# Feed-forwards that begin with half the tokens, memory keys beside the products, mixing norms two steps forward

## The chip, the cores and the metric

The kernel runs on one core of one Trainium2 chip. The metric is device time in microseconds (us), from launch to end, as the median of several executions; lower is better. Five engines work side by side and wait for each other through semaphores: PE (TensorE, matrix products and transposes), DVE (VectorE) and ACT (ScalarE) for elementwise work, POOL (almost idle here) and SP, which only issues transfers (DMA) here.

## The reference

One layer of a decoder over 1024 tokens of width 1024, all in f32, with pre-normalisation everywhere (`rmsnorm(x, g) = x * rsqrt(mean(x*x) + eps) * g`):

```python
h = x + 0.5 * swiglu(rmsnorm(h, ffn1_norm), w_gate, w_up, w_down)      # feed-forward 1, width 2816
u = rmsnorm(h, mix_norm)
(fq, fk, fv, ff, dq, dk, dv, iq, ik, iw, mq, g) = split(u @ w_in)
o_a = fox_attention(fq, fk, fv, logf)                                  # causal, with forget bias
o_b = dsa_attention(dq, dk, dv, iq, ik, iw, k_sel)                     # top-k keys by an indexer
km, vm = split(rmsnorm(mem, mem_norm) @ w_mem_kv)                      # 256 memory tokens
o_c = memory_attention(mq, rmsnorm(km, mem_k_norm), vm)
h = h + (sum_i sigmoid(g_i) * (o_i @ w_branch_i)) @ w_out
h = h + 0.5 * swiglu(rmsnorm(h, ffn2_norm), ...)                       # feed-forward 2
# swiglu(x, wg, wu, wd) = (silu(x @ wg) * (x @ wu)) @ wd
```

## The kernel before

Every f32 factor of a product is split into a high part (a rounded copy that PE takes at full rate, made by an ACT cast) and a low part (the rest, made by a DVE subtraction), and a product is three matmuls: high by high, high by low, low by high. In the rows `wH`, `wL` are the parts of weights (rings of four buffers, fed by staging tiles `wS`), `th`, `tl` those of activations, `nT` the PSUM tile that a transpose fills, and a 128x512 matmul is the unit of nearly all work.

**Feed-forward.** `FeedForward.first_half` computes gate and up, `second_half` the down product. Both use a fast scheme with seven half-size products in place of eight. For gate and up the token-side factors are seven tiles of 128 x (4 x 512), made once per feed-forward by `Combos`: B11 and B21 are the first 512 tokens (rows 0 to 3 of eight rows of 128 tokens), lower and upper half of the width; B12 and B22 are the last 512 tokens (rows 4 to 7); T3 = B22 - B12, T2 = T3 + B11, T1 = B12 - B11, T4 = B21 - T2. The weight-side sums are the tiles `S`, made by DVE for each job (`prep_sums`, `prep_split`). A job is one 2 x 128-column piece of gate or up; there are 22 jobs, each of seven products (`product`), each product of 12 matmuls. The map from product to token tile is

```python
RIGHT = {1: B11, 2: B21, 3: B22, 4: T4, 5: T1, 6: T2, 7: T3}
```

and a job goes 1, 2, 6, 5, 7, 3, 4. The results of a job pass through PSUM banks `gx`, `gy` into an SBUF tile `gu` by ACT copies and DVE additions. Jobs 0 and 1 are interleaved product by product, as their token tiles become ready; the others follow each other.

**Before feed-forward 1** the kernel of before normalises and turns (transposes) the memory rows, multiplies them by `w_mem_kv` (96 matmuls, tile `tm`, consumers `mem_keys` and `mem_values`), and between these normalises the rows of x in pairs (t, t+4), `x_pair`, each pair turned by `Combos.sums`, which writes all of the token tiles for those 128 columns. Only when all four pairs are through do `open_high` and `first_half` begin: the first product waits for all eight rows.

**Before feed-forward 2** the product with `w_out` runs over the eight token rows in the order 0, 4, 1, 5, 2, 6, 3, 7 (consumer `residual`), each row is normalised as it ends, and the pairs are turned in the same way.

**Between feed-forward 1 and the mixing**, `second_half` calls `beside(i, y)` at its last steps (42 steps in all; i = 0 at step 30). At i = 8 to 11 it normalises rows 0 to 3 for the mixing (`to_mix`, `norm_rows`: a scale, eight transposes into free PSUM banks, a split); at i = 11 it issues the loads of the narrow projection's weights (`nb.fetch`). After the second half come row 3's rest, the narrow projection (tile `nar`, 192 matmuls of 128x256) and, as filler, gate products.

The order of work is the order of issue in the program, smoothed by a scheduler within each engine; a planner class (`_Flow`) keeps estimated clocks only to choose which of several chains is issued next. Engines run their own lists in order.

Of the kernel before, what the change touches and what calls it, by code (L numbers as in the profile page):

```python
# [19 lines left out]
P = 128  # L20
# [135 lines left out]
def trunk_layer_kernel(  # L156
# [133 lines left out]
    def normalise(tp, out, row, gain):  # L290
        v = tp.tile([P, 1], F32, tag="nv", name="nv", bufs=3)
        junk = out
        if out is row:
            junk = tp.tile([P, D], BF16, tag="njunk", name="njunk", bufs=1)
        A.activation(junk, row, AF.Square, accum_out=v)
        y = rsqrt_mean(tp, v, D)
        V.scalar_tensor_tensor(out, row, y[:, 0:1], gain, op0=OP.mult, op1=OP.mult)


    def norm_rows(tp, row, gain, uh, ul, t, free=None, sq=None):  # L300
        sq = sq() if sq else tp.tile([P, D], F32, tag="nsq", name="nsq", bufs=2)
        normalise(tp, sq, row, gain)
# [18 lines left out]
    class Block:  # L321


        def __init__(self, bp, srcs, ncols, bufs=4, tag="b", out=None):
            self.bp, self.srcs, self.ncols, self.bufs, self.tag, self.out = bp, srcs, ncols, bufs, tag, out
            self.ws, self.ready = [None] * len(srcs), [0.0] * len(srcs)
# [8 lines left out]
        def step(self, uh, ul, t, consume, after=None):  # L335
# [7 lines left out]
            for k in range(NK):  # L343
                wh, wl = self.ws[k // kper]
                wh, wl = wh[:, k % kper], wl[:, k % kper]
                a, b = uh[:, k, t * P:(t + 1) * P], ul[:, k, t * P:(t + 1) * P]
# [34 lines left out]
    class Combos:  # L381


        def __init__(self):
            self.lp = pool("tl", side="right")
            self.low = [self.lp.tile([P, 4, 512], F32, tag=f"t{i}", name="raw", bufs=1) for i in range(7)]

        def open_high(self):
            self.hp = pool("th", side="right")
            high = self.hp.tile([P, 8, 4, 512], F32R, name="th")  # L390
            self.high = [high[:, i] for i in range(7)]
            self.spare = lambda: high[:, 7]


        def sums(self, tp, t, ra, rb):
            sl = slice(t * P, (t + 1) * P)
            bs = []
            for r in (ra, rb):
                for c in range(2):
                    pt = bank("nT")  # L400
                    for k in range(4):
                        T.transpose(pt[:, k * P:(k + 1) * P], r[:, (4 * c + k) * P:(4 * c + k + 1) * P], ident)
                    bs.append(pt.rearrange("p (k t) -> p k t", k=4))
            b11, b21, b12, b22 = bs
            low = [x[:, :, sl] for x in self.low]
            x12 = tp.tile([P, 4, P], F32, tag="x12", name="x12", bufs=1)
            A.copy(x12, b12)
            A.copy(low[B11], b11)
            V.tensor_sub(low[T3], b22, x12)
            A.copy(low[B21], b21)  # L410
            V.tensor_sub(low[T1], x12, b11)
            A.copy(low[B22], b22)
            V.tensor_add(low[T2], low[T3], b11)
            V.tensor_sub(low[T4], b21, low[T2])


        def split(self, i):
            hi, raw, self.low[i] = self.high[i], self.low[i], self.spare()
            A.copy(hi, raw)
            V.tensor_sub(self.low[i], raw, hi.bitcast(F32))  # L420
            self.spare = lambda: self.lp.tile([P, 4, 512], F32R, tag=f"t{i}", name="tl", bufs=1)

        def release(self):
            self.hp.release()
            self.lp.release()

    class FeedForward:
        def __init__(self, combos, w_gate, w_up, w_down, residual):
            self.staged, self.ready = {}, {}
            self.c, self.wgu, self.wd, self.residual = combos, (w_gate[0], w_up[0]), w_down[0], residual  # L430
            self.raw, self.jobs, self.n_jobs = {}, {}, 2 * HF
# [11 lines left out]

        def fetch(self, j):
            if j < self.n_jobs and j not in self.raw:
                p, w = j // 2, self.wgu[j % 2]
                rs = []
                for f in (p, p + HF):
                    r = slot([P, NK, P], F32, "wS")
                    load(r, w[:, f * P:(f + 1) * P].rearrange("(k p) f -> p k f", p=P))  # L450
                    rs.append(r.rearrange("p (a k) f -> p a (k f)", a=2))
                self.raw[j] = rs

        def job_of(self, j):
            if j not in self.jobs:
                self.jobs[j] = self.tp.tile([P, 4, 512], F32, tag="S", name="S", bufs=2), {}
            return self.jobs[j]

        def prep_sums(self, j, part):
            ra, rb = self.raw[j]  # L460
            s = self.job_of(j)[0]
# [7 lines left out]
        def prep_split(self, j, g):  # L469
            ra, rb = self.raw[j]  # L470
            s, d = self.job_of(j)
            v, names = ((ra, (1, 2)), (s[:, 0:2], (6, 5)), (s[:, 2:4], (7, 3)), (rb[:, 1:2], (4,)))[g]
# [4 lines left out]
        def product(self, pt, j, n, start):  # L477
            sh, sl = self.jobs[j][1][n]
# [6 lines left out]
        def job(self, j):  # L485
            gate = j % 2 == 0
            u = self.tp.tile([P, 4, 512], F32, tag="gu", name="gu", bufs=3)
# [12 lines left out]
            x = tagged_bank("x", 2, "gx")  # L500
            self.product(x, j, 1, True)
            yield
            y = tagged_bank("y", 4, "gy")
            self.product(y, j, 2, True)
# [5 lines left out]
            y = tagged_bank("y", 4, "gy")  # L510
# [19 lines left out]
            del self.raw[j], self.jobs[j]  # L530


        def first_half(self):
            fl.sync()
            self.tp = pool("ffa")
            c = self.c
            for j in range(2):
                self.fetch(j)
                self.prep_split(j, 0)
            pair = [self.job(0), self.job(1)]  # L540

            def step(split=(), groups=()):
                for i in split:
                    c.split(i)
                for g in pair:
                    next(g)
                for g in groups:
                    for j in range(2):
                        self.prep_split(j, g)

            c.split(B11)
            step()
            c.split(B21)
            for j in range(2):
                self.prep_sums(j, 0)
                self.prep_split(j, 1)
            step((T2,))
            step((T1,))
            for j in range(2):
                self.prep_sums(j, 1)  # L560
                self.prep_split(j, 2)
            step((T3,))
            step((B22,), (3,))
            self.fetch(2)
            self.fetch(3)
            step((T4,))
            for part in range(2):
                self.prep_sums(2, part)
                self.prep_split(2, part)
            step()  # L570
            self.prep_split(2, 2)
            last = pair
            for j in range(2, self.n_jobs):
                g, n = self.job(j), j + 1
                for st in range(7):
                    next(g)
# [210 lines left out]
    def head_norm(tp, pt, nh, bufs=4):  # L787
        hd = 512 // nh
        sq = tp.tile([P, 512], F32, tag="hx", name="hsq", bufs=bufs)
# [30 lines left out]
    def mem_keys(tp):  # L820
        def consume(t, pt):
            xn = head_norm(tp, pt, 4, 2)
            yield
            for i, v in enumerate(turn(tp, xn)):
                store(km_s[:, :, i].rearrange("h p m -> p h m")[:, :, t * P:(t + 1) * P], v)
        return consume

    def mem_values(tp):
        def consume(t, pt):
# [883 lines left out]
```

## Time and profile before

| | |
|---|---|
| median of 3 runs | 2542.94 us (2538.59 to 2545.95) |
| profiled execution, its own time | 2544.91 us |
| its span, first to last instruction | 2542.9 us |
| PE busy | 2419.0 us, 95% |
| DVE, ACT busy | 64%, 45% |
| instructions | 31538 |

How to read it: the span is the profiled execution's time less 2.0 us that lie outside its instructions. PE is busy nearly all the time, so time can only be won where PE waits or where its clock is low; the waits lie at a few places, and the rows further down show three of them.

### The profile page before, as it was taken

Reading aid. Unit: us, or ns where it says so; the run is one execution under the profiler, and the core shown is the slowest. Engines: PE = TensorE matmul, PEld = TensorE weight load, DVE = VectorE, ACT = ScalarE, POOL = GpSimd, SP = SyncE. Lnnn points to the kernel's source line nnn. Section 1 sums busy time; section 2 is a strip of 40 time slices with the busy share of each in tenths; the row PEclk is TensorE's granted clock in tenths of the full one; section 3 lists DMA queues with packets and bytes.
Section 4 is the critical chain, followed back from the end, with each engine's and each line's share of the span. In section 5 each row is a group of like instructions: output and inputs, shape, how many; then the busy total and the mean of one; then the engine's idle time right before and its main releaser. Section 6 shows DMA issues by size and latency. Waiting matters only on the chain.

```text
span 2542.9 us, 31538 instructions
## 1 busy us (share of the span) xinstructions
PE 2419.0 (95%) x11532; PEld 2001.3 (79%) x11532; DVE 1617.0 (64%) x3201; ACT 1147.4 (45%) x1904; POOL 2.2 (0%) x40
## 2 busy tenths in 40 slices
PE   6999999999999999989899998999979999999998
PEld 4788888888787877778688886877768888888887
DVE  7755555488757588584565556777376555554885
ACT  5533333333433277768865555543144333333332
POOL 0000000000000000000000000000000000000000
PEclk9999999999999999999899999999989999999999
DMA  7222222474334534544455535757422222225743
GB/s 233 75 84 77 88 86 79 157 303 137 128 114 138 156 116 137 151 155 146 132 148 141 149 107 182 233 172 232 175 75 67 91 75 84 91 77 192 269 152 126
DMA packets 297899, 351.63 MB, mean 138 GB/s; under 512 B 18792, under 2 KB 199688, under 8 KB 297744
## 3 DMA queue, kind: packets, MB, share of 16 engines
q1 hardware_dynamic: 297744, 349.62, 42.8%
q8 instruction: 90, 1.47, 0.2%
q14 instruction: 65, 0.53, 0.1%
HBM read 254.98 MB, written 93.54 MB: 137 GB/s over the span
## 4 chain that ended last, share of the span: by engine, by line
PE 79%; DVE 9%; ACT 6%; DMA 3%; issue 3%; SPq 0%; ACTq 0%; DVEq 0%
PE gx L51 19%; PE gy L51 14%; PE tm L51 9%; PE gate L51 8%; PE dx L51 8%; PE dy L51 7%; PE br L51 4%; ACT junk L51 3%; PE po L51 2%; PE pT L51 2%; PE sp L51 2%; DVE wL L51 2%; PE nar L51 1%; PE isc L51 1%; DMA wS<-in_w_in 1%
## 5 line engine op out<-in xcount | busy, mean ns | idle before, releaser
L51 ACT CAST wH<-wS 128x1024 fp32r<-128x1024 f32 x238 | 225.6, 953 | 304.7 <-PE gy L51 103.0
L51 PE MATMUL gx<-th,wH 128*128 128x512 f32 x880 | 317.4, 393 | 7.2 <-ACT th L51 7.2
L51 DVE TENSOR_TENSOR wL<-wS,wH 128x1024 fp32r<-128x1024 f32 x238 | 260.3, 1099 | 98.3 <-ACT wH L51 93.8
L51 PE MATMUL gx<-th,wL 128*128 128x512 f32 x704 | 274.9, 390 | 0.0
L51 PE MATMUL gy<-th,wH 128*128 128x512 f32 x528 | 206.3, 391 | 1.2 <-ACT th L51 1.2
L51 PE MATMUL gy<-tl,wH 128*128 128x512 f32 x528 | 205.4, 389 | 0.0
L51 PE MATMUL gx<-tl,wH 128*128 128x512 f32 x528 | 205.4, 389 | 0.0
L51 PE MATMUL gy<-th,wL 128*128 128x512 f32 x528 | 205.4, 389 | 0.0
L51 PE MATMUL tm<-wH,uh 128*128 128x512 f32 x496 | 199.8, 403 | 3.1 <-ACT wH L51 3.1
L51 PEld LDWEIGHTS gx<-th,wH 128*128 128x128 f32 x880 | 166.9, 190 | 42.8 <-ACT th L51 8.0
L51 PE MATMUL tm<-wL,uh 128*128 128x512 f32 x496 | 196.5, 396 | 2.1 <-DVE wL L51 1.3
L51 PE MATMUL tm<-wH,ul 128*128 128x512 f32 x496 | 196.5, 396 | 0.0
L51 ACT ACTIVATE junk<-wk,sn 128x384 bf16<-128x384 f32 (+5 forms) x186 | 164.2, 883 | 64.6 <-DVE sn L51 55.4
L51 ACT CAST wH<-S 128x1024 fp32r<-128x1024 f32 x88 | 92.4, 1051 | 171.2 <-PE gy L51 167.9
L51 DVE TENSOR_TENSOR wL<-S,wH 128x1024 fp32r<-128x1024 f32 x88 | 107.5, 1223 | 87.3 <-ACT wH L51 87.3
L51 DVE TENSOR_TENSOR gu<-gu,gy 128x512 f32<-128x512 f32 x88 | 60.3, 686 | 157.0 <-PE gy L51 85.3
L51 DVE TENSOR_TENSOR pl<-pT,ph 128x512 fp32r<-128x512 f32 (+1 forms) x176 | 109.5, 637 | 78.9 <-ACT ph L51 77.8
L51 PE MATMUL gate<-uh,wH 128*128 128x512 f32 x384 | 156.0, 406 | 0.0
L51 PEld LDWEIGHTS gx<-th,wL 128*128 128x128 f32 x704 | 133.0, 189 | 27.8
L51 PE MATMUL gate<-uh,wL 128*128 128x512 f32 x384 | 152.5, 397 | 0.0
L51 PE MATMUL gate<-ul,wH 128*128 128x512 f32 x384 | 152.0, 396 | 0.0
L51 PE MATMUL dx<-wH 128*128 128x512 f32 x352 | 137.5, 391 | 3.5 <-DVE rows L51 2.5
(261 smaller groups left out, 5160.9 us busy)
## 6 DMA issues: line engine op xcount, KB each, us to landing
wS<-in_ffn_w_down SPq DMA_DIRECT2D x70, 512.0 KB, 4.7
wS<-in_w_in SPq DMA_DIRECT2D x48, 512.0 KB, 4.0
wS<-in_ffn_w_gate SPq DMA_DIRECT2D x44, 512.0 KB, 3.9
wS<-in_ffn_w_up SPq DMA_DIRECT2D x44, 512.0 KB, 3.7
hid_s<-gu SPq DMA_DIRECT2D x44, 512.0 KB, 3.0
a<-hid_s SPq DMA_DIRECT2D x30, 512.0 KB, 9.5
g_s<-sg SPq DMA_DIRECT2D x48, 256.0 KB, 2.4
bg<-g_s SPq DMA_DIRECT2D x48, 256.0 KB, 3.1
```

The lines of the kernel that those rows point to most:

```text
L51: return fn(*a, **k)
```

## The change

1. `normalise` takes a list of rows with one chain of small rsqrt operations for all of them; rows of x are now normalised in pairs (0,1), (2,3), (4,5), (6,7).
2. Both feed-forwards begin with products 1 and 2 of jobs 0, 1 and 2 (`first_products`, `second_products`, 72 matmuls), which need only rows 0 to 3. Rows 4 to 7 are normalised and turned while these run. `Combos.first(t)` copies a row's two halves into B11 and B21; `Combos.second(t)` makes T3 and T2 per row; T1 and T4 are made later as whole tiles of 128 x 2048 (`rest`). B11 and B21 are split in quarters, T2 in halves (`split(i, parts)`).
3. Memory keys and values are no longer made before feed-forward 1. A generator `mem_kv` is advanced once per product of jobs 4 and up in feed-forward 1's gate and up part; it takes staging tiles from the ring `S`, weight parts from the rings `wH`, `wL`, and two PSUM banks. It issues 12 matmuls at a time between products, at eight places. To make room `gu` has two buffers instead of three in this feed-forward, and `gy` three banks instead of four.
4. `w_out` goes through the rows in order 0 to 7 in feed-forward 2's beginning; row 7's sum and normalisation come after the first products are issued.
5. `beside` starts two steps earlier: norms at i = 6 to 10, narrow weights at i = 9, the first gate weights at i = 10 and 11. Staging tiles for these rows come from the other pool `wx`.

```diff
+    def normalise(tp, outs, rows, gain, tag="njunk", bufs=1):
+        v = tp.tile([P, n], F32, tag="nv", name="nv", bufs=3)
+        for i, (out, row) in enumerate(zip(outs, rows)):
...
+            A.activation(junk, row, AF.Square, accum_out=v[:, i:i + 1])
         y = rsqrt_mean(tp, v, D)
-        V.scalar_tensor_tensor(out, row, y[:, 0:1], gain, op0=OP.mult, op1=OP.mult)
+        for i, (out, row) in enumerate(zip(outs, rows)):
+            V.scalar_tensor_tensor(out, row, y[:, i:i + 1], gain, op0=OP.mult, op1=OP.mult)
...
+        def first(self, t, row):
             sl = slice(t * P, (t + 1) * P)
+            for i, b in zip((B11, B21), self.turned(row)):
+                A.copy(self.raw[i][:, :, sl], b)
+        def second(self, t, row):
+            b12, b22 = self.turned(row)
+            raw = {i: x[:, :, t * P:(t + 1) * P] for i, x in self.raw.items()}
+            A.copy(raw[T1], b12)
+            V.tensor_sub(raw[T3], b22, raw[T1])
+            A.copy(raw[B22], b22)
+            V.tensor_add(raw[T2], raw[T3], raw[B11])
+        def rest(self, i):
+            r = self.raw
+            if i == T1:
+                V.tensor_sub(r[T1], r[T1], r[B11])
+            else:
+                r[T4] = r[T2]
+                V.tensor_sub(r[T4], r[B21], r[T2])
...
+        def first_products(self):
+            self.three = [self.job(j, True) for j in range(3)]
+            for g in self.three:
+                next(g)
+        def second_products(self, beside):
+            for i, g in enumerate(self.three):
+                next(g)
+                beside(i)
...
+                    if beside and j > 3:
+                        self.st = st
+                        next(beside, None)
...
+    def mem_kv(ff):
+        stage = lambda: ff.tp.tile([P, 4, 512], F32, tag="S", name="mS", bufs=2)
...
+                for half in range(2):
+                    yield from until((4, 6)[half])
+                    wh, wl = ff.split2(e[:, 2 * half:2 * half + 2])
+                    yield from until((5, 0)[half])
+                    if acc is None:
+                        acc = [bank("kv") for t in range(2)]
+                    for t in range(2):
+                        for k in range(2):
...
+                            mm3(acc[t], [(a, wh[:, k]), (a, wl[:, k]), (b, wh[:, k])], kt == 0, kt == NK - 1)
...
-    fl.run(order + kv[3:], width=3)
...
+    nm(0, 1)
+    combos.first(0, rows[0])
+    combos.first(1, rows[1])
+    nm(2, 3)
+    ff.begin(1)
+    combos.first(2, rows[2])
+    combos.first(3, rows[3])
+    combos.split(B11, 4)
+    ff.begin(3)
+    ff.first_products()
+    ff.rest()
+    combos.split(B21, 4)
+    nm(4, 5)
+    nm(6, 7)
...
+    ff.second_products(halves)
     nmp.release()
-    ff.first_half()
+    ff.first_half(mem_kv(ff))
...
-        if i == 6:
+        if i == 5:
...
-        if i >= 8:
-            next(m["norms"][i - 8])
-        if i >= 9:
-            next(m["norms"][i - 9], None)
-        if i == 11:
+        if 6 <= i <= 9:
+            next(m["norms"][i - 6])
+        if 7 <= i <= 10:
+            next(m["norms"][i - 7], None)
+        if i == 9:
...
-        consume.order = (0, 4, 1, 5, 2, 6, 3, 7)
...
+    combos.split(B11, 4)
+    combos.split(B21, 4)
+    total(NT - 1, final[0])
...
+    ff.first_products()
+    ff.rest()
+    normalise(tp, [h[NT - 1]], [h[NT - 1]], gain3)
+    ff.second_products(lambda i: combos.second(3, h[NT - 1]) if i == 0 else None)
```

How the engines' lists move, at the places that the prediction speaks of. First PE's list at its very start (`nsq` is a scaled memory row, `xt` a row of x, `mh` the turned memory, `th_117` the parts of B11); minus is before, plus is after:

```order
-L1709 UNCONDITIONAL_BRANCH
-L51 MATMUL nT<-ident,nsq 128x128 x16
-L51 MATMUL tm<-wH,mh 128x512
+L1842 UNCONDITIONAL_BRANCH
+L51 MATMUL nT<-ident,xt 128x128 x32
+L51 MATMUL gx<-th_117,wH 128x512 x4
+L51 MATMUL gx<-th_117,wL 128x512
```

PE no longer begins with the memory rows and their product; it turns four rows of x and goes straight into feed-forward products. Next DVE's list in the same stretch of the program after the change, from the last token rows to the parts that product 6 needs (`raw_112` is T3, `raw_110` T2, `nT_429` the turned row 7, `th2_119` T2's parts, `S_450` and `S_457` the weight sums of jobs 0 and 1):

```order
L51 TENSOR_TENSOR raw_110<-raw_112,raw_108 128x4x128
L51 TENSOR_TENSOR raw_112<-nT_429,raw_111 128x4x128
L51 TENSOR_TENSOR S_450<-wS_295 128x512
L51 TENSOR_TENSOR raw_110<-raw_112,raw_108 128x4x128
L51 TENSOR_TENSOR S_450<-S_450,wS_136 128x512
L51 TENSOR_TENSOR S_457<-wS_297 128x512
L51 TENSOR_TENSOR gu_442<-gu_442,gy_343 128x512
L51 TENSOR_TENSOR S_457<-S_457,wS_138 128x512
L51 TENSOR_TENSOR gu_444<-gu_444,gy_370 128x512
L51 TENSOR_TENSOR th2_119<-raw_110,th2_119 128x1024 x2
L51 TENSOR_TENSOR wL_454<-S_450,wH_453 128x1024
L51 TENSOR_TENSOR wL_461<-S_457,wH_460 128x1024
```

Between the last row's T3 and T2's low half stand four weight sums and two `gu` additions. In the middle of feed-forward 1's gate and up part, PE's list after the change at the first of the eight `mem_kv` steps (`kv` is a PSUM bank of keys, `left` and `ml` the turned memory's high and low parts):

```order
L51 MATMUL gy<-raw,wH 128x512 x2
L51 MATMUL gy<-raw,wL 128x512
L51 MATMUL kv<-wH,left 128x512
L51 MATMUL kv<-wL,left 128x512
L51 MATMUL kv<-wH,ml 128x512
L51 MATMUL kv<-wH,left 128x512
```

These stand between one product's last matmul and the next product's first, and need parts of weights that come through the same rings. Last, the beginning of feed-forward 2. PE's list before: the last matmuls of `w_out`, then 32 transposes, then products (`h_15893` holds all eight rows):

```order
L51 MATMUL tm<-wL,uh_15389 128x512
L51 MATMUL tm<-wH,ul_15390 128x512
L51 MATMUL nT<-ident,h_15893 128x128 x32
L51 MATMUL gx<-th,wH 128x512 x2
L51 MATMUL gy<-th,wH 128x512 x2
```

and DVE's list after the change at that place (`h2_6`, `h2_7` are rows 6 and 7, `wL_16495` to `wL_16503` the first weights' low parts, `th0` and `th1` the parts of B11 and B21):

```order
L51 TENSOR_TENSOR wL_16495<-wS_16465,wH_16494 128x1024
L51 SCALAR_TENSOR_TENSOR rs_a_16453<-rs_a_16453,nv_16448 128x1
L51 TENSOR_TENSOR wL_16499<-wS_16467,wH_16498 128x1024
L51 SCALAR_TENSOR_TENSOR rs_y_16452<-rs_a_16453,rs_y_16452 128x1
L51 SCALAR_TENSOR_TENSOR h2_6_15836<-h2_6_15836,rs_y_16452,gain_row_15849 128x1024
L51 TENSOR_TENSOR wL_16503<-wS_16463,wH_16502 128x1024
L51 TENSOR_TENSOR raw_15825<-nT_16511,raw_15824 128x4x128
L51 TENSOR_TENSOR raw_15825<-nT_16525,raw_15824 128x4x128
L51 TENSOR_TENSOR raw_15823<-raw_15825,raw_15821 128x4x128 x2
L51 TENSOR_TENSOR th0_16538<-raw_15821,th0_16538 128x512 x4
L51 TENSOR_TENSOR th1_16539<-raw_15822,th1_16539 128x512 x4
L51 TENSOR_TENSOR h2_7_15837<-h2_7_15837,tm_16469 128x512
```

Row 7 is now scaled behind B11's and B21's low parts, and only 24 transposes stand behind the last `w_out` matmul (rows 5, 6 and 7).

## Rows read from the trace of the kernel before

**Rows 1.** The page: span, busy time of each engine
```profile
span 2542.9 us, 31538 instructions
...
PE 2419.0 (95%) x11532; PEld 2001.3 (79%) x11532; DVE 1617.0 (64%) x3201; ACT 1147.4 (45%) x1904; POOL 2.2 (0%) x40
...
```

**Rows 2.** Chain that ended last, first feed-forward: start, length, engine and tile
```profile
...
2.59 7.69 DMA xt<-in_x
...
49.89 5.49 PE tm L51 x24
...
72.27 6.41 PE gx L51 x22
...
116.31 2.72 PE gx L51 x12
...
488.94 2.73 PE gx L51 x12
...
```

**Rows 3.** Windows: start to end, length, busy by engine, clock, DMA share, GB/s
```profile
...
20.00:36.00 16.00, 12.07 (x56) 9.58 (x54) 13.56 (x38) 10.61 (x17) 0.00 (x0) 0.94 0.79 260
36.00:41.00 5.00, 1.22 (x6) 1.09 (x6) 5.00 (x30) 0.58 (x1) 0.00 (x0) 0.50 0.97 279
41.00:45.00 4.00, 4.00 (x12) 3.08 (x11) 2.90 (x11) 0.59 (x1) 0.00 (x0) 0.58 0.30 72
...
84.00:490.00 406.00, 406.00 (x1793) 336.30 (x1792) 219.74 (x280) 142.88 (x196) 0.00 (x0) 1.00 0.28 86
...
```

**Rows 4.** Waits of PE before 72 us: total, times, longest
```profile
...
PE nT L51 <- DVE identb L208: 8.7, 1, 8.7
...
PE gx L51 <- ACT th L51: 3.6, 1, 3.6
...
```

**Rows 5.** DVE by form before 72 us: count, busy, mean ns, idle before
```profile
...
L51 DVE TENSOR_TENSOR wL<-wS,wH 128x1024 fp32r<-128x1024 f32 x10 | 12.1, 1219 | 0.0
L51 DVE SCALAR_TENSOR_TENSOR xt<-xt,rs_y,gain_row 128x1024 f32<-128x1024 f32 x8 | 10.2, 1279 | 0.1
L51 DVE SCALAR_TENSOR_TENSOR rs_y<-rs_a,rs_y 128x1 f32<-128x1 f32 x20 | 2.9, 155 | 0.3
L51 DVE TENSOR_TENSOR raw<-nT,raw 128x512 f32<-128x512 f32 x4 | 2.7, 687 | 0.1
...
L51 DVE TENSOR_TENSOR th<-raw,th 128x2048 fp32r<-128x2048 f32 x1 | 2.3, 2293 | 0.0
...
```

**Rows 6.** ACT by form before 72 us
```profile
...
L51 ACT CAST wH<-wS 128x1024 fp32r<-128x1024 f32 x10 | 10.3, 1056 | 0.6 <-PE tm L51 0.6
L51 ACT ACTIVATE njunk<-xt 128x1024 bf16<-128x1024 f32 x8 | 8.5, 1058 | 4.0 <-DMA xt<-in_x 3.9
L51 ACT COPY raw<-nT 128x512 f32<-128x512 f32 x12 | 6.8, 592 | 4.3 <-DVE raw L51 3.0 <-PE nT L51 1.3
...
```

**Rows 7.** Timeline of PE, start of the second feed-forward: start, length, idle before
```profile
...
1882.25 1.91 PE L51 MATMUL nT<-ident,h 128*128 128x128 f32 x16
1887.17 1.58 PE L51 MATMUL nT<-ident,h 128*128 128x128 f32 x8 [3.02 <-DVE h L51]
1896.92 1.97 PE L51 MATMUL nT<-ident,h 128*128 128x128 f32 x8 [8.16 <-DVE h L51]
1902.50 1.22 PE L51 MATMUL gx<-th,wH 128*128 128x512 f32 x2 [3.62 <-ACT th L51]
...
```

**Rows 8.** Chain, end of the second feed-forward's gate and up products
```profile
...
2322.05 2.73 PE gx L51 x12
...
```

**Rows 9.** Windows, start of the mixing and of the second feed-forward
```profile
...
713.00:725.00 12.00, 11.13 (x67) 10.87 (x67) 5.64 (x11) 5.34 (x7) 0.00 (x0) 0.72 0.61 201
1876.00:1930.00 54.00, 38.63 (x173) 31.27 (x172) 42.99 (x60) 32.82 (x39) 0.00 (x0) 0.81 0.15 50
...
```

**Rows 10.** Waits of PE at the start of the mixing
```profile
...
PE nar L51 <- ACT wH L51: 4.6, 1, 4.6
...
```

**Rows 11.** Chain around the last steps of the first feed-forward
```profile
...
659.83 6.88 DMA wS<-in_ffn_w_down
...
```

More of the change, by code (lines that the diff above doesn't have):

```diff
@@ L417, in split @@
[L417 to L421, printed above, removed]
+            self.hp = pool("th")
+            pairs = [self.hp.tile([P, 2, 4, 512], F32R, name=f"th{i}") for i in range(4)]
+            th = [x[:, i] for x in pairs for i in range(2)]
+            self.place = {B11: th[0:2], B21: th[2:4], T2: th[4:6], T1: th[6:8], T3: (B11, T1), B22: (T4, T3),
+                          T4: (B21, B22)}
@@ new lines, in split, with left @@
+        def split(self, i, parts=1):
+            raw = self.raw[i]
+            hi, lo = self.high[i], self.low[i] = [
+                self.old(x, F32R) if isinstance(x, int) else x for x in self.place[i]]
+            n = 4 // parts
+            for k in range(0, 4, n):
+                A.copy(hi[:, k:k + n], raw[:, k:k + n])
+                V.tensor_sub(lo[:, k:k + n], raw[:, k:k + n], hi[:, k:k + n].bitcast(F32))
+        def left(self, shape, dtype):
+            return self.lp.tile(shape, dtype, tag=f"t{T2}", name="left", bufs=1)
@@ new lines, in mem_kv @@
+        for k in range(NK):
+            load(gm[:, k:k + 1], mem_norm[0, k * P:(k + 1) * P].unsqueeze(1))
+        mh = ff.c.left([P, NK, MEM], F32R)
+        ml = ff.tp.tile([P, NK, MEM], F32R, name="ml")
+        yield from until(2)
+        e = stage()
+        rows = [e[:, 2 * t:2 * t + 2].rearrange("p a d -> p (a d)") for t in range(2)]
+        for t in range(2):
+            load(rows[t], mem[t * P:(t + 1) * P, :])
+        yield from until(5)
+        v = ff.tp.tile([P, 2], F32, name="mv")
@@ L1244, in trunk_layer_kernel @@
-    mnorm = [chain(norm_rows(nmp, rows[t], mgain, mh, ml, t)) for t in range(2)]
-    def x_pair(t):
-        pair = []
-        for r in (t, t + 4):
-            row = nmp.tile([P, D], F32, tag="xt", name="xt", bufs=4)
-            load(row, x[r * P:(r + 1) * P, :])
-            pair.append(row)
-        fl.t += 3.0
-        for row in pair:
-            yield
-            normalise(nmp, row, row, gain)
-        yield
-        combos.sums(nmp, t, *pair)
-    xnorm = [chain(x_pair(0)), chain(x_pair(1), mnorm), chain(x_pair(2)), chain(x_pair(3))]
@@ L1354, in trunk_layer_kernel @@
     sgp = pool("sgp", side="right")
[L1355 to L1357 removed]
+    gates = mixing["gates"]
     gates.tp = sgp
```

366 lines of the change are left out of this document (202 added, 164 removed).

## The prediction

> **What bounds the kernel now.** I read the page first: PE is busy 2419.0 of 2542.9 us [rows 1], so what the change can win is PE's idle time and the time its clock is low, at three places; what it can lose is new waits. Then I read the chain that ended last, to see what the three places are in time, the windows, to see how much of each stretch PE works and at which clock, and the waits of PE, to see what it waits for.
>
> In feed-forward 1's gate and up part a product of 12 matmuls takes 2.72 us and PE never pauses: 406.00 busy of 406.00 from 84 to 490 us, clock 1.00 [rows 2, 3]. The part ends at 488.94 + 2.73 = 491.7 [rows 2]. Its 22 x 7 = 154 products need 154 x 2.72 = 418.9; 96 memory matmuls at 5.49 per 24 need 21.9 [rows 2]; 88 transposes (16 memory, 8 keys, 64 token), at 1.91 per 16 or 0.12 each [rows 7], need 10.6. Sum 451.4. So 40.3 us of the first 491.7 are lost, all before about 78 us, where the chain first runs smoothly [rows 2]. In this stretch PE waits 8.7 at once for the first transposes and 3.6 for the first product's `th` [rows 4], and it has the low level of the clock for a while: 0.50 from 36 to 41, in which PE worked 1.22 of 5 us, and still 0.58 in the next 4 us, in which it worked without a pause [rows 3].
>
> In feed-forward 2 the last `w_out` matmul ends at 1882.25, and the last gate and up product at 2322.05 + 2.73 = 2324.8 [rows 7, 8]: 442.5 us. The work in it is 418.9 + 32 transposes of 0.12 = 422.7, so 19.8 are lost: waits of 3.02, 8.16 and 3.62 [rows 7], and a clock of 0.81 on average in the window around [rows 9].
>
> At the mixing's start PE waits 4.6 for the narrow weights' cast [rows 10] and then works 12 us at a mean clock of 0.72 [rows 9], which costs 12 x 0.28 = 3.4.
>
> **Edit 1 to 3, feed-forward 1.** I placed the new instructions by the order shown above and gave each its duration.
> To the first product: the fifth 512 KB load issued lands at 2.59 + 7.69 = 10.3 [rows 2]. Now the first five are x rows 0, 1, the gain, rows 2, 3, so rows 2 and 3 are there at 10.3. Then two squares of 1.06 with 0.2 behind each [rows 6] (the 0.2 is my allowance), 2.5; nine small operations at 0.155 [rows 5] and a little issue, 1.6; two scales at 1.28 [rows 5], 2.6; sixteen transposes, 1.9 [rows 7]; an evacuation, 0.6 [rows 6], and a quarter of B11's cast, half of that. First product at 20.0.
> Then 72 matmuls (16.3) and 32 transposes (3.8) follow; the clock is low for the first of them as in 41 to 45, which cost 4 x 0.42 = 1.7 [rows 3]. DVE must in the same time make three weights' low parts (3.7 at 1.22), eight quarters of `th0`, `th1` (5.5 at 0.69, the 128x512 row), eighteen small operations and four scales (8): 17, so PE sets this stretch. It ends at 41.8.
> Now a new wait: T2 can only be finished when row 7 is turned. From there DVE's list has the rest of the token rows (4 x 0.69 = 2.75), four weight sums (2.75), two `gu` additions (1.4) and half of T2's low part (1.2), behind an ACT copy of 0.6 [rows 5, 6]: 8.7 us. Product 6 starts at 50.5. After it 148 products (402.6), 96 memory matmuls (21.9) and 24 transposes (2.9) remain, 427.4. I add 1.7 for the low clock after the wait [rows 3], 1.2 for T1, whose whole-tile subtraction and low part cost 2.3 each [rows 5] behind the wait on the sums, and 3.0 for the eight memory steps: their weights' cast (1.06) and low part (1.22) [rows 5, 6] start when an earlier product gives the ring's buffer back, one product or 2.7 to 3.2 us before the step needs them, so a step waits 0 to 0.6; I take 0.4. End at 50.5 + 433.3 = 483.8 against 491.7: **7.9 gained**. Bounds: 12 where the memory steps and the T1 wait cost nothing and a T2 wait is 2 us shorter; a loss of 13 where each memory step stalls PE for 3 us more than assumed (8 x 2.6 = 21).
> The extra work on DVE and ACT lies beside PE in this part: 219.74 and 142.88 busy of 406 [rows 3]. The transfers do too: the DMA share there is 0.28, so 4 MB of memory weights more are a small thing; without that cover each would cost its 1 to 2 us.
>
> **Edit 4, feed-forward 2.** From the last `w_out` matmul: 24 transposes (2.9) and 154 products (418.9). Waits: row 6's scale stands behind two weights' low parts, 1.1; B11's first low quarter behind row 6's scale, a weight's low part and four token operations, (1.28 + 1.22 + 2.75 less what PE turns meanwhile) 3.3; for T2 and the second job's weights, 0.3 + 1.2; for T1, whose subtraction, four sums and low part (2.3 + 2.75 + 2.3 by [rows 5]) stand ahead, less the product running, 4.8. Two spells of low clock of 1.7 each [rows 3]. Sum 14.1 against 19.8, and the work is 0.9 less behind that matmul but as much in all, so **5.7 gained** from this. Bounds: 0 (each of DVE's chains a third longer) to 12 (half the waits hidden).
>
> **Edit 5, the mixing's start.** The loads go out two steps, 2 x 5.1 us (42 steps in 490 to 706), earlier, so the 4.6 wait and the 3.4 of low clock [rows 9, 10] go, and 0.9 behind them: 8.9. The norms' transposes now lie between products, as many as before. New: row 6's square stands behind a cast on ACT, about 2 (1.06 each) [rows 6]. And at step 36 row 0's scale now stands on DVE in the place where the transfers of down weights are late already (6.88 us, [rows 11]); the product behind it may wait another 0 to 5, I take 2. **5 gained**, bounds -2 and 9.
>
> The middle of the kernel (attention) gets the same work, but 24 gate matmuls move from the mixing's start into it as filler; 24 x 0.23 = 5.5 us either way is a bound, and I take 0.
>
> **Sum.** 7.9 + 5.7 + 5.0 = 18.6. From the profiled execution's own time 2544.91 this gives 2526.3; that execution is 2.0 above the median of the runs, 2542.94, so against the median the time is 2524.3. A measurement of this kernel can tell about 0.3%, 7.6 us, from no change.
>
> **A page that speaks against it.** The trace's row: after a stretch with little work, the next 4 us of gapless matmuls still had clock 0.58 [rows 3]. The Trainium skill, "TensorE: Matmul & The Clock Gate", Part 1: The HAM clock gate, says that the throttled state is the default and activity releases it; the trace agrees. I charged this at three of the new waits. By that rule every one of the seven waits that I place, short ones too, could be followed by a low clock; whether the short ones are, the rows do not show. By the rule taken so far, four more at 1.7 are 6.8 us, the time 2531.
>
> **The rivals.**
> *A, the forecast*: 2524, with its own range 2515 to 2533. Chance 0.50.
> *B, low clock behind each wait and DVE's chains a third longer*: DVE is the engine named in most of these waits, and in 36 to 41 it was busy 5.00 of 5 [rows 3]. The waits of 8.7, 3.3 and 4.8 grow by 5.6, the clock by 6.8: 12 lost, 2536. Against it: most of DVE's operations in the new waits have known durations. Chance 0.16.
> *C, the memory steps stall the products*: each step's weight parts take a ring buffer that the next job's parts want, so these come late too, by about a product, 2.7 us a step; 8 x 2.7 = 21.6 and the whole gain is gone: 2546, no change. For it: the margin of 2.7 to 3.2 against 2.3 of work is thin; against it: 35% of ACT's and 54% of DVE's time is used there [rows 3]. Chance 0.13.
> *D, slower*: the same place, but with the `gu` ring of two buffers late as well, so that a step costs two products, 5.4: 43 us lost against 18.6 gained, 2567. It is slower than before by more than 0.3% from 3.3 us a step on ((18.6 + 7.6) / 8). Chance 0.08.
> *E, the change wins more*: the waits for T2 and T1 overlap with products that the scheduler moves ahead, and the gate filler fills attention's waits: 12 + 9 + 9, 2513, and to 2508 with the filler's 5.5. Chance 0.13.
>
> **The numbers.** Faster by over 0.3% (below 2535.3): A, E, and not quite half of B, 0.71; slower (above 2550.6): D and a part of C, 0.11; the same 0.18. The forecast is 2524. A range from 2510 to 2546 leaves out D, part of C and the end of E, together 2 in 10.
>
> **What would show it.** Right: PE's first product near 20 us, a wait of about 9 near 42, gapless products with 12 `kv` matmuls at eight places, the gate and up part ending near 484; in feed-forward 2 three waits of 1 to 5 us, and about 436 us from the last `w_out` matmul to the last product; no wait of `nar` for `wH`. Wrong: `kv` or `gx` waiting for `wH` or `wL` several times (C, D), a clock below 1.00 in windows after 84 us (B), or a wait in the second half at step 36 above 5 us.

## The result, and the profile after

The changed kernel took 2514.74 us (median of 4 runs, 2512.44 to 2521.56), the kernel before, on the same chip, 2541.39 (4 runs, 2538.59 to 2545.95): ratio 0.9898, 95% interval 0.9872 to 0.9923. A second set on another chip gave 2520.61 against 2542.91, ratio 0.9911 (0.9897 to 0.9925). The forecast was 2524, faster, in a range from 2510 to 2546.

The page of the changed kernel, its first lines, against [rows 1]:

```profile
span 2519.5 us, 31509 instructions
...
PE 2419.0 (96%) x11532; PEld 1998.8 (79%) x11532; DVE 1619.4 (64%) x3162; ACT 1149.5 (46%) x1918; POOL 2.2 (0%) x40
```

PE's busy time, in which a matmul at the low clock counts with its longer time, is the same to a tenth of a microsecond. So in this pair the 23.4 us by which the span is shorter (2542.9 less 2519.5) are pauses of PE; low clock that went at one place came at another. In the second profiles of both kernels, told further on, the busy time differs by 6.9 of 31.8 us (2422.4 and 2415.5). To see where the time went, read when PE begins each stage in both traces (us; first matmul of the next stage, or end of the last one of the tile named):

| stage mark | before | after | gained in the stage |
|---|---|---|---|
| feed-forward 1: end of gate and up | 491.50 | 483.32 | 8.2 |
| second half and mixing's start, to the indexer's first product (`isc`) | 861.34 | 834.76 | 18.4 |
| attention, to the last `br` | 1786.58 | 1766.45 | -6.5 |
| `w_out` and feed-forward 2's gate and up, to the last `gx` | 2324.78 | 2301.98 | 2.7 |
| last down product | 2536.87 | 2513.45 | 0.6 |

The second and third lines belong together: 24 gate matmuls of 0.23 us moved from the one to the other (5.5 us), so the mixing gained about 13, the middle lost about 1, 12 in sum. Forecast were 7.9, 5.0, 0 and 5.7 for the first four.

**Feed-forward 1.** Windows of the changed kernel (start to end, length, busy by engine, clock, DMA share, GB/s), against [rows 3]:

```profile
20.00:42.00 22.00, 21.30 (x100) 17.44 (x100) 16.57 (x38) 11.44 (x21) 0.00 (x0) 1.00 0.21 39
42.00:51.00 9.00, 2.54 (x8) 1.42 (x8) 8.30 (x12) 8.88 (x11) 0.00 (x0) 0.76 0.00 0
51.00:55.00 4.00, 3.95 (x12) 2.95 (x12) 4.00 (x4) 0.96 (x3) 0.00 (x0) 0.68 0.00 0
...
90.00:480.00 390.00, 390.00 (x1733) 322.62 (x1732) 214.03 (x298) 140.77 (x194) 0.00 (x0) 1.00 0.31 97
```

PE is busy from 20 to 42, pauses for 6.24 us and once more for 1.6 near 60, and from 90 on works without a gap for 390 us at full clock, although the memory product's steps now lie in between. In the timeline of PE (start, length, what, idle before and its releaser), the longer pause is the one for T2:

```profile
42.22 0.65 PE L51 MATMUL nT<-ident,xt 128*128 128x128 f32 x4 [0.68 <-ACT raw L51]
49.11 2.17 PE L51 MATMUL gx<-th,wH 128*128 128x512 f32 x4 [6.24 <-ACT wH L51]
```

It is released by ACT's cast of a weight sum, not by DVE. The timeline of ACT in the same stretch shows the list ahead of that cast:

```profile
43.70 0.58 ACT L51 COPY raw<-nT 128x512 f32<-128x512 f32 x1
44.32 1.90 ACT L51 CAST raw<-raw 128x2048 fp32r<-128x2048 f32 x1
46.12 1.99 ACT L51 CAST th<-raw 128x1024 fp32r<-128x1024 f32 x2
48.02 1.99 ACT L51 CAST wH<-S 128x1024 fp32r<-128x1024 f32 x2
```

The whole-tile cast at 44.32 is that of B22, which a job needs only after two further products (5 and 7); T2's casts and the weight sums' stand behind it. The chain that ended last closes the part at 480.77 + 2.72 = 483.5, where [rows 2] had 491.7:

```profile
480.77 2.72 PE gx L51 x12
```

**The mixing's start.** `nar` waits for nothing any more ([rows 10] had 4.6); the first narrow product starts at 702.50 instead of 712.74. The waits of SP (its transfers' queue) from 656 to 716 us tell when the weights' loads could go out. First the kernel before, then after (total, times, longest; L176 is a store, L173 a load):

```profile
SPq L176 <- DVE rows L51: 40.6, 1, 40.6
...
SPq L173 <- PE dy L51: 1.1, 1, 1.1
```

```profile
SPq L173 <- PE dy L51: 18.6, 2, 13.8
SPq L173 <- DVE wS L51: 14.8, 1, 14.8
```

And the loads in SP's timeline, before and after:

```profile
707.29 3.13 SPq L173 DMA_DIRECT2D wS<-in_w_in  x6
```

```profile
687.26 16.45 SPq L173 DMA_DIRECT2D wS<-in_w_in  x9
```

Before, SP stood 40.6 us at the store of row 4 of `h`, which is ahead in its list, and then for the transposes (`dy<-ident,wS`) that hold the staging tiles. After, the store is behind the first loads, and SP stands ahead of them for a DVE operation on such a tile (14.8) and for such transposes (13.8 at the longest), which now lie two steps earlier. Counted from the first down product (491.50 and 483.32) the loads go out at 203.9 us instead of 215.8.

**Feed-forward 2.** Waits of PE from 1865 to 1910 us, where [rows 7] had 3.02, 8.16 and 3.62:

```profile
PE gx L51 <- DVE th L51: 2.8, 1, 2.8
PE gy L51 <- DVE th L51: 1.9, 1, 1.9
PE gy L51 <- ACT th L51: 1.6, 1, 1.6
PE gx L51 <- DVE wL L51: 0.5, 1, 0.5
PE nT L51 <- DVE h L51: 0.4, 1, 0.4
```

7.2 us in five waits for 14.8 in three; the mean clock from 1876 to 1930 is 0.93, against 0.81 in [rows 9].

### The profile page after: what moved, and what is told of

The parts are those of the page before. It is cut to its first block, busy times and chain, and to the rows that moved or that the text cites. A ratio compares the mean times of both kernels' runs of the same rounds, so it can differ in the third digit from the quotient of the medians.

```text
span 2519.5 us, 31509 instructions
## 1 busy us (share of the span) xinstructions
PE 2419.0 (96%) x11532; PEld 1998.8 (79%) x11532; DVE 1619.4 (64%) x3162; ACT 1149.5 (46%) x1918; POOL 2.2 (0%) x40
## 4 chain that ended last, share of the span: by engine, by line
PE 74%; DVE 11%; ACT 6%; DMA 6%; issue 3%; SPq 0%; ACTq 0%; DVEq 0%
PE gx L51 18%; PE gy L51 14%; PE tm L51 8%; PE dx L51 7%; PE gate L51 7%; PE dy L51 7%; PE br L51 3%; PE po L51 3%; ACT junk L51 2%; PE sp L51 2%; DVE wL L51 2%; PE pT L51 2%; DMA wS<-in_ffn_w_down 1%; PE nar L51 1%; PE kv L51 1%
## 5 line engine op out<-in xcount | busy, mean ns | idle before, releaser
L51 ACT CAST wH<-wS 128x1024 fp32r<-128x1024 f32 (+1 forms) x230 | 217.0, 949 | 300.3 <-PE gy L51 76.4
L51 DVE TENSOR_TENSOR wL<-wS,wH 128x1024 fp32r<-128x1024 f32 (+1 forms) x230 | 250.6, 1095 | 108.7 <-ACT wH L51 105.2
L51 PE MATMUL gx<-th,wH 128*128 128x512 f32 x704 | 222.7, 398 | 10.3 <-ACT wH L51 6.2
L51 PE MATMUL gx<-raw,wH 128*128 128x512 f32 x704 | 217.0, 389 | 0.6 <-DVE gu L51 0.6
L51 PEld LDWEIGHTS gy<-th,wH 128*128 128x128 f32 x704 | 133.7, 191 | 34.8 <-DVE th L51 4.4
L51 PEld LDWEIGHTS gx<-raw,wH 128*128 128x128 f32 x704 | 132.0, 188 | 28.6 <-DVE gu L51 1.1
L51 PE MATMUL tm<-wH,uh 128*128 128x512 f32 x368 | 148.5, 405 | 3.3 <-ACT wH L51 3.3
L51 PE MATMUL tm<-wH,ul 128*128 128x512 f32 x368 | 145.7, 396 | 0.0
L51 PE MATMUL gx<-th,wL 128*128 128x512 f32 x352 | 138.9, 395 | 0.6 <-DVE wL L51 0.5
L51 PE MATMUL gy<-th,wL 128*128 128x512 f32 x352 | 138.7, 394 | 0.0
```

The source lines that it names most:

```text
L51: return fn(*a, **k)
```

## The experiments

Three things were open: whether the gain in feed-forward 1 comes from beginning with half the tokens or from the memory product's leaving the head; which part of edit 5 made the mixing gain more than twice what was forecast (the weights' place, the norms' place, or the moved gate matmuls); and whether half-beginnings matter in feed-forward 2. All times are ratios to the kernel before on the same chip, with 95% intervals.

**Feed-forward 1 without the half-beginning.** All eight rows are turned first; B11 and B21 are made to depend on T2's last column by adding 0 times it, so that no product starts sooner.

```diff
+    t2 = combos.raw[T2][:, :, 511:512]
+    for i in (B11, B21):
+        b = combos.raw[i][:, :, 0:1]
+        V.scalar_tensor_tensor(b, t2, 0.0, b, op0=OP.mult, op1=OP.add)
     combos.split(B11, 4)
...
-    ff.second_products(halves)
+    ff.second_products(lambda i: None)
```

> The changed kernel, but in feed-forward 1 no product begins before all eight rows are turned (a tiny operation makes B11 and B21 depend on row 7). The memory work stays beside the products. If beginning with half the tokens is what shortened the head, the first product comes at about 31 us and the gate and up part ends later than 483.3 by up to 11: 2518 to 2526. Rival: the half beginning only moves the wait (T2 needs row 7 anyway), and the gain is that the memory product left the head: first product near 31, no wait for T2, end of gate and up at 476 to 481, 2508 to 2513.

Measured: 0.9916 (0.9899 to 0.9932); by its whole time this kernel can't be told from the changed one, so the reading goes by the stage. The timeline of PE has the first product at 39.62 (some 31 was expected) instead of 20.00:

```profile
39.62 1.65 PE L51 MATMUL gx<-th,wH 128*128 128x512 f32 x3 [3.92 <-ACT th L51]
```

T2's wait is gone, and the part ends at 487.07. In eight profiles with the half-beginning, the same cast of B22 and the memory matmuls once it ends between 482.8 and 483.9. So the half-beginning is worth 3.75 of the 8.2 us, though it starts the products 19.6 us sooner. Of the rest, 3.8 are the 32 transposes that this kernel has behind it by then, and 9.0 are waits of the changed kernel from its first product on (6.24, 1.59, 0.68, 0.24, 0.22). The last 3 are not placed: low clock explains little of them, for this kernel has it too behind its wait of 3.92 (0.50 from 39.6 to 44, 0.84 to 50). The other 4.4 remain without the half-beginning; they come with the memory product's leaving the head and the paired norms, which were not parted further.

**The memory matmuls twice.** Each of the 96 is issued a second time.

```diff
+                            for r in range(2):
-                            mm3(acc[t], [(a, wh[:, k]), (a, wl[:, k]), (b, wh[:, k])], kt == 0, kt == NK - 1)
+                                mm3(acc[t], [(a, wh[:, k]), (a, wl[:, k]), (b, wh[:, k])],
+                                    kt == 0 and r == 0, kt == NK - 1 and r == 1)
```

> The changed kernel with each of the 96 memory matmuls issued twice (memory values come out twice as large). If these matmuls cost their own time and nothing more, the gate and up part of feed-forward 1 ends 96 x 0.227 = 21.8 us later, at 505.1, with no wait of PE between 90 and 500 us. Rival: the steps also make the next products' parts late; then waits of 0.5 us and more show at several of the eight places and the end is later than 508.

Measured, in a single run: 2543.09. The gate and up part ends at 506.01, 22.7 later, for 96 x 0.23 = 22 us of matmuls, and PE still does not pause. Window of this kernel:

```profile
90.00:500.00 410.00, 410.00 (x1821) 339.26 (x1820) 213.01 (x296) 142.09 (x196) 0.00 (x0) 1.00 0.29 92
```

The extra matmuls cost their own time and little else; the steps' casts, low parts and loads were not doubled, and they make no product wait in either kernel.

**Feed-forward 2 without the half-beginning.** Row 7 is summed and normalised like the others, and all rows are turned before the first product.

```diff
         if t == NT - 1:
             ff.begin()
-            final.append(pt)
-            return
         total(t, pt)
...
-    normalise(tp, [h[NT - 1]], [h[NT - 1]], gain3)
-    ff.second_products(lambda i: combos.second(3, h[NT - 1]) if i == 0 else None)
+    ff.second_products(lambda i: None)
```

> The same in feed-forward 2: row 7 is normalised and turned before the first product, the order 0 to 7 of the rows stays. If beginning with half counts, the time from the last w_out matmul to the last gate and up product grows from 436.9 by 2 to 6: 2517 to 2521. Rival: one wait of some 5 us before the first product takes the place of five smaller ones (7.9 together and their low clock): 433 to 436, 2511 to 2515.

Measured: 0.9898 (0.9882 to 0.9915). The waits of PE have one long one of 9.9 us for `h` in place of the other four:

```profile
PE nT L51 <- DVE h L51: 10.3, 2, 9.9
```

From the last `br` to the last `gx` it takes 528.9 us, and 533.8 and 533.2 in two later kernels without the half-beginning; the changed kernel took 535.5 and 530.9 in two profiles, seven other kernels with the half-beginning between 528.6 and 534.7, the kernel before 538.2 and 540.6. The half-beginning is worth nothing that these runs can tell here. What feed-forward 2 gains is in this version too, so it must lie in what the two share: `w_out`'s rows in order, the tiles' new making, or what the list of the change does not name, that `h` is now eight tiles of one row and no longer one of all rows. Which of these it is was not tried.

**Edit 5 undone.** Norms at i = 8 to 11, narrow weights at i = 11, no early gate weights.

```diff
-        if 6 <= i <= 9:
-            next(m["norms"][i - 6])
-        if 7 <= i <= 10:
-            next(m["norms"][i - 7], None)
-        if i == 9:
+        if i >= 8:
+            next(m["norms"][i - 8])
+        if i >= 9:
+            next(m["norms"][i - 9], None)
+        if i == 11:
...
-        if i >= 10:
-            m["gates"].fetch(i - 10)
```

> The changed kernel with edit 5 undone (norms for the mixing at i = 8 to 11, narrow weights at i = 11, first gate weights after the second half, as before). By the step of the prediction it loses 5 us against the changed kernel: about 2520. By the two traces the stretch from the second half's first matmul to the first indexer score was 18.4 us shorter, of which some 5.5 are gate products that only moved; if edit 5 made all of it, it loses 11 to 14: 2526 to 2529. Rival: the shorter stretch has little to do with edit 5 (other waits fell differently): under 3 us.

Measured: 0.995 (0.9931 to 0.997). Edit 5 alone carries about half of the whole gain. One part of it stays in this kernel: by the diff it is rows 4 to 7, normalised after the second half, that stage in the pool `wx`; rows 0 to 3 use the ring of the weights before and after. The loads of the narrow weights stand ahead of the store of row 4 here, and still go out at 699.37, 216.6 us from the first down product, as before the change; so it was not the store that held them.

**Its two halves apart.** In the first kernel only the norms are put back to i = 8 to 11, and the weights stay at i = 9. In the second only the weights are put back:

```diff
-        if i == 9:
+        if i == 11:
...
-        if i >= 10:
-            m["gates"].fetch(i - 10)
```

> The changed kernel with only the norms of edit 5 put back (i = 8 to 11); narrow weights and gate weights stay early. If the early loads of the narrow weights are what counts, it is within 2 us of the changed kernel (2515) and shows no wait of nar for wH of 4 us. If the norms' place counts, it comes near the kernel with all of edit 5 undone.

> The changed kernel with the narrow weights and the first gate weights late again (i = 11), the norms early. If the two waits stand one behind the other (narrow weights and row 3's norm), putting back either one alone loses most of edit 5: a wait of nar for wH of 3 to 5 us and a low clock behind it, 6 to 12 us longer than the changed kernel. If only the norms' place counts, within 3 us of the changed kernel.

Measured: norms late 0.9949 (0.9927 to 0.9971); weights late 0.9906 (0.9892 to 0.9919). The norms' place decides; that of the weights makes no difference that these runs can tell. In the second kernel's timeline of SP the loads go out at the same time as in the changed kernel, though they stand two steps later in the program:

```profile
687.51 14.08 SPq L173 DMA_DIRECT2D wS<-in_w_in  x8
```

SP waits there for `PE dy` as well (18.5 us, 2 times): a load goes when the transposes give back its staging tile. With the norms late and the weights early, the first load does go out early, at 661.56, but the weights now take the tiles from the norms. Timeline of PE in that kernel:

```profile
710.89 1.97 PE L51 MATMUL dy<-ident,wS 128*128 128x128 f32 x8 [6.44 <-DVE wS L51]
714.88 0.58 PE L51 MATMUL nar<-wH,uh 128*128 128x256 f32 x1 [2.02 <-DVE ul L51]
```

**The norms one step later.** i = 7 to 10 for the first part, 8 to 11 for the second.

```diff
-        if 6 <= i <= 9:
-            next(m["norms"][i - 6])
-        if 7 <= i <= 10:
-            next(m["norms"][i - 7], None)
+        if 7 <= i <= 10:
+            next(m["norms"][i - 7])
+        if 8 <= i <= 11:
+            next(m["norms"][i - 8], None)
```

> The changed kernel with the norms for the mixing one step later (i = 7 to 11 in place of 6 to 10), all else the same. If row 0's scale in front of the late down weights makes the waits of 1.6 and 2.6 at step 36, these shrink to the 1.9 and 0.6 of the kernel before. If the narrow weights' loads wait for the staging tiles of these norms, they go out some 5 us later than at 687, and a wait of nar for wH under 3 us may come back. Net: within 4 us of the changed kernel either way.

Measured: 0.9964 (0.9951 to 0.9976). One step of 5 us costs as much as the whole edit brings, against 4 us expected at most, and the waits at step 36 are no shorter (3.4 and 1.9). The loads go out at 695.15. The last norm row is too late for PE again:

```profile
708.43 1.25 PE L51 MATMUL dy<-ident,wS 128*128 128x128 f32 x8 [4.25 <-DVE wS L51]
...
712.74 0.58 PE L51 MATMUL nar<-wH,uh 128*128 128x256 f32 x1 [3.06 <-DVE ul L51]
```

**The gate matmuls put back.** 24 gate matmuls are issued behind the narrow projection again, as before the change.

```diff
+    while gates_f.n < 4:
+        fl._step(gates_f)
```

> The changed kernel with 24 gate matmuls put back behind the narrow projection, ahead of the wide projections (60 there, as before). If these 24, left over as filler, are what filled the waits of turn in the wide projections (3.25 and 2.1 before, 0.95 after), those waits and the low clock behind them come back: 3 to 6 us longer. Rival: the waits went because rows are normed earlier: no difference beyond 2 us.

Measured: 0.9902 (0.9888 to 0.9915). The middle takes 925.95 instead of 931.69 us, and the stretch from the first down product to the first `isc` 355.3 instead of 351.4: what the middle lost is these matmuls, and they are no cause of the gain ahead of it.

From the first down product to the last `br` the gates make no difference, so this stretch shows edit 5 by itself (us):

| kernel | first `dy` to last `br` |
|---|---|
| before, two profiles | 1295.1, 1298.4 |
| edit 5 undone | 1293.3 |
| norms late; norms one step later | 1300.2; 1298.1 |
| changed, two profiles | 1283.1, 1287.1 |
| weights late; gates put back | 1287.6; 1281.2 |
| five other kernels with edit 5 whole | 1280.3 to 1288.4 |

**Finer steps in feed-forward 1, and a combination.** B22 is split in quarters, so that T2's casts need not stand behind one of 1.90 us; feed-forward 2 is that without the half-beginning. The second kernel has the gates put back as well.

```diff
-            c.split(B22)
+            c.split(B22, 4)
```

> The changed kernel with feed-forward 2 as in the run with all rows first, and B22's cast in feed-forward 1 in four parts instead of one of 128 x 2048 (1.9 us), which stood ahead of T2's casts on ACT. If ACT's list sets the wait for T2, it shrinks from 6.24 to some 5 us and the gate and up part ends 1 to 2 us earlier; with the 2 us of feed-forward 2 the time is 2 to 4 us below the changed kernel. If DVE's list sets it, as the prediction said, the wait stays above 6.

> The changed kernel with three edits that did no harm alone: all rows before the products in feed-forward 2, B22's cast in four parts, 24 gate matmuls behind the narrow projection. If their small gains add (1.5 us in the gate and up part of feed-forward 1, 0 to 3 in the two others), 0.987 to 0.990 of the kernel before, against 0.990 to 0.991 of the changed kernel; the gate and up part ends at 481.9 again. Rival: the two others only moved by chance from run to run: no better than 0.990.

Measured: 0.9896 (0.9882 to 0.991) and 0.9895 (0.9878 to 0.9911). The timeline of ACT in the first of them shows one quarter ahead of T2's casts and three behind the weight sum's:

```profile
44.33 0.62 ACT L51 CAST raw<-raw 128x512 fp32r<-128x512 f32 x1
44.91 1.99 ACT L51 CAST th<-raw 128x1024 fp32r<-128x1024 f32 x2
46.81 1.04 ACT L51 CAST wH<-S 128x1024 fp32r<-128x1024 f32 x1
...
49.70 1.64 ACT L51 CAST raw<-raw 128x512 fp32r<-128x512 f32 x3
```

PE's wait for that cast falls from 6.2 to 5.0, with a new one of 1.0 for `wL`, and the part ends at 481.86 instead of 483.32. That ACT's list sets the T2 wait is thus shown, with DVE's close behind it; the 1.5 us are too few to show in the time, and neither kernel can be told from the changed one.

**Both kernels once more**, for a second profile of each.

> The changed kernel itself, as the mark for the three others on the same chip: 0.99 of the kernel before.

> The kernel before once more, for a second profile: its stages within 2 to 3 us of those of the first (gate and up of feed-forward 1 ends at 491.5, second half to the first indexer score 369.8, w_out and feed-forward 2's gate and up 538.2).

The changed kernel is the second set told with the result. The kernel before, in a single run, took 2552.37, longer than nine other runs of it on that chip (2542.44 to 2548.40); its stages are used above as a second reading, with that in mind.

## Why the prediction was right, and where not

**Direction and size.** Forecast 18.6 us against the profiled execution, measured 23.4; by medians 2514.7 against 2524. That is a shade below case A's own range (2515 to 2533) and next to E's 2513; the second set's 2520.6 lies inside it. E's reasons did not come about: the middle lost 1 us, and the waits for T2 and T1 were not hidden behind products. It was A, with one term too small; in the profiled pair a smaller gain from edit 4 hid a part of that.

**Edits 1 to 3: right.** 7.9 forecast, 8.2 measured. The first product at 20.0 stands in the trace as 20.00; the end was forecast at 483.8 and came, by the same mark, at 483.5. That it agrees to 0.3 is in part luck. Within it the T2 wait was 6.2 instead of 8.7, and the step that put DVE's list in charge was wrong: ACT's cast released it. The wait for T1 (1.2) came as 1.6 for a token tile near 60. The 3.0 for memory steps were not needed at all, nor the 1.7 of low clock charged to the first products (1.00 from 20 to 42). Against that the first stretch still ended 1.1 us late (42.9 for 41.8), and from T2's product to the end it took 434.4, where the forecast without the memory steps has 430.3: more low clock than charged (0.68 in two windows), a longer T1 wait, and a rest that was not placed.

**Rivals C and D: wrong.** Not one wait between 90 and 480 us, and none with the memory matmuls doubled. The margin of one product is enough here.

**Rival B: half of its mechanism.** Low clock does follow waits that I had taken as harmless. Windows of the changed kernel behind the waits of 1.6 (near 60), 1.6 and 2.6 (664 and 668), 2.8 (1870), 0.5 (1894) and 1.9 (1901):

```profile
59.00:63.00 4.00, 3.24 (x9) 2.59 (x10) 4.00 (x4) 2.56 (x3) 0.00 (x0) 0.68 0.46 128
668.00:672.00 4.00, 3.70 (x10) 2.97 (x11) 4.00 (x6) 1.31 (x3) 0.00 (x0) 0.57 0.00 0
...
1870.00:1874.00 4.00, 3.52 (x8) 2.81 (x9) 4.00 (x8) 1.71 (x4) 0.00 (x0) 0.50 0.13 39
1894.00:1898.00 4.00, 2.69 (x11) 1.80 (x10) 4.00 (x5) 2.92 (x4) 0.00 (x0) 1.00 0.01 4
1901.00:1905.00 4.00, 3.54 (x8) 2.81 (x9) 4.00 (x4) 1.91 (x2) 0.00 (x0) 0.50 0.50 145
```

Where it is low, it costs about what the forecast charged for one, 4 x 0.3 to 0.5 us; the wait of half a microsecond is not followed by one. But the length of a wait does not settle it. In the second profile of the changed kernel the same wait of 2.8 is followed by the full clock:

```profile
1874.60:1890.00 15.40, 15.40 (x72) 12.86 (x73) 11.03 (x24) 6.36 (x12) 0.00 (x0) 1.00 0.09 36
```

And in the kernel before, a wait of 1.85 at 673 is (1.00 from 672 to 690). The Trainium skill, "TensorE: Matmul & The Clock Gate", Part 1: The HAM clock gate, makes the throttled state the default that activity releases; the trace agrees behind these waits of 1.6 us and more in the profiled execution (0.50 to 0.68), and not behind the one of 0.5 (1.00), nor in the two places just named. DVE's chains, the other half of B, did not grow.

**Edit 4: near in size, not in cause.** 5.7 forecast; 2.7 in the profiled pair, and with a second profile of each kernel between 2.7 and 9.6 (538.2 and 540.6 less 535.5 and 530.9). By the prediction's own mark, from the last `w_out` matmul to the last product, about 436 were forecast; 436.9 and 432.2 came, for 442.4 before. More than half of the difference between the two is the low clock behind the wait of 2.8, which one has (0.81 from 1870.5 to 1886) and the other has not. What the mark leaves out is `w_out` itself, which took 98.6 us instead of 95.8, 0.9 of it for transposes that moved there; the prediction had no loss there. The waits are 7.2 us against 10.7 placed. But the prediction worked its waits out for beginning with half the rows, and the version without that gains as much.

**Edit 5: the term that was mis-sized.** 5 forecast, about 12 measured, middle included. The 8.9 us of waits and low clock that were to go did go: `nar` has no wait, and the clock from 690 to 730 is 1.00. What was added at step 36 was charged about rightly (4 in all): waits of 1.6 and 2.6 where the kernel before had 2.5 in two, and low clock behind them, 4 x 0.43. Timeline of PE after the change:

```profile
664.60 1.09 PE L51 MATMUL dy<-ident,wS 128*128 128x128 f32 x8 [1.59 <-DVE wS L51]
668.30 0.77 PE L51 MATMUL dx<-wH 128*128 128x512 f32 x1 [2.60 <-DVE rows L51]
```

Missing from the sum was what lies 50 us further on, in the wide projections. Waits of PE from 725 to 866 us, before, then after, then with edit 5 undone:

```profile
PE turn L51 <- DVE rs_y L51: 5.3, 2, 3.3
```

```profile
PE turn L51 <- DVE rs_y L51: 1.0, 1, 1.0
```

```profile
PE turn L51 <- DVE rs_y L51: 4.8, 2, 3.3
```

With the low clock behind them before (0.72 from 776 to 786, 10 x 0.28 = 2.8; 1.00 from 725 to 834 after) these are 7 us. They go with edit 5: 4.8 with it undone, 3.5 and 4.1 with the norms late, 2.3 with the weights late, 1.2 with the gates put back. Which of DVE's operations come earlier was not isolated.

The step's reason was wrong too. That the loads go out "two steps, 2 x 5.1 us" earlier is right in size (11.9), but the prediction had it from the loads' place in the program. With the norms early, that place made no difference that the runs can tell, and the norms', which the prediction treated as neutral ("as many as before"), decided.

**The middle: 0 forecast, -1 measured.** The gates are neutral, as assumed. One new wait was not foreseen. Timeline of PE, the window ahead of it, and the chain that ended last:

```profile
1556.43 0.79 PE L51 MATMUL br<-wH 128*128 128x512 f32 x1 [10.40 <-ACT wH L51]
```

```profile
1540.00:1557.00 17.00, 1.99 (x5) 1.32 (x6) 10.67 (x18) 6.50 (x10) 0.00 (x0) 0.55 0.80 253
```

```profile
1551.58 3.73 DMA wS<-in_w_branch
```

The branch weights' load is issued at 1551.58, behind loads of `o_s`, while PE has nothing else. The second profile has it too (10.9), the kernel before 2.6. With the gates put back the longest wait for these weights is 2.7 again, and the middle 5.7 us shorter, which the gates' own 5.5 explains; so the one long wait stands in place of smaller ones. The windows bear that out: in the 66 us up to the first `br` PE is idle 17.0 us after the change and 8.6 before, from there to the last `br` 4.6 and 11.6. With the gates put back it is 8.7 and 11.4, so the trade comes with the moved gate matmuls.

## What to carry to other kernels

Before moving a load forward, see in the transfer queue's waits what it waits for: if it waits for a tile that some other chain holds, move that chain, and the load's own place in the program may not matter. When a step is moved ahead, check every later stage that the same engine serves, and not only the wait that the step ends in; a step of 5 us decided 13 here. Beginning a stage with the half of the data that is ready brings little if the second half's arrival then stalls the engine: 20 us of earlier start became 3.75, and at the other place nothing that could be measured.

## What was not expected of the hardware

The low clock followed pauses of PE as short as 1.6 us here, at a place where a longer one lay some 10 us back (0.68 in 59 to 63) and where two had 0.7 us of work between them (1.6 and 1.9 near 1900, 0.50), while it stayed at 1.00 behind one of 0.5. Nor is it the same each time: the wait of 2.8 near 1870 was followed by 0.50 in one profile of the changed kernel and by 1.00 in the other, so a forecast can charge such a spell only with a chance. And 96 matmuls with their weight parts, casts and loads, and 192 with the same parts, fitted between products without a single wait, with DVE busy 52 to 55% and ACT 35 to 36% of the stretch.
